# A seventh fast tile pair in the FFN's second product, with the weight sums of three tiles kept in DRAM

## The chip, the cores and the metric

The kernel runs on one core of a Trainium2 chip. The metric is the device time of one execution in microseconds; lower is better.

## The reference

The reference is one decoder block of a hybrid network on 256 tokens of width 1024: two token mixers and an output projection, then a SwiGLU FFN with a hidden width of 2816, each followed by a residual and a LayerNorm. All is float32. The change touches the FFN:

```python
h = jnp.einsum('bsd,df->bsf', x, w_ffn_in)
h_gate, h_up = jnp.split(h, 2, axis=-1)
y = jnp.einsum('bsf,fd->bsd', jax.nn.silu(h_gate) * h_up, w_ffn_down)
return layer_norm(DN_ALPHA * x + y, ln2_w, ln2_b)
```

## The kernel before

**Numbers in two parts.** TensorE multiplies in fp32r, which has fewer digits than float32. Each operand is therefore held as a high part h (a copy cast to fp32r) and a low part l (the operand less h), and a product is three matmuls: h with h, h with l, l with h. Weights come from DRAM in tiles of 128 x 2048 float32 (1 MB). For each tile, SP issues the load into a raw buffer (three of them, taken in turn), ScalarE casts it to `wh` (L204), and VectorE subtracts to make `wl` (L206). There are four h buffers and four l buffers, also taken in turn: the fifth tile can be cast only when TensorE has finished the first. `plan()` (L77) lists the tiles in their order, `loads` (L169) turns that into steps, and `fetch()` (L238) writes the steps into the program up to three ready tiles ahead of the one being used.

**The FFN's first product.** `ffn_step(j)` (L881) takes two feature blocks of the gate and two of the up half: two weight tiles, 32 matmuls each (L293 with 512 columns, L294 with 256). The results are copied out of PSUM by ScalarE (L887) and VectorE (L888), silu is taken and the activations are split into h and l. A scheduler sets the order of the steps up to `NF - 2 * ORDERED`; the last two steps and the second product are in the order in which they are written.

**The FFN's second product.** The hidden width makes eleven tile pairs q = 0 to 10: one weight tile of 256 rows by 1024 columns each. A plain pair (P) multiplies two row blocks by two token halves and two column halves: 8 products, 24 matmuls of 512 columns (`rows_pass`, L721). A fast pair (S) treats the tile as a 2 x 2 block matrix and needs 7 products, 21 matmuls (`fast`, L921). In exchange it needs sums of the tile's four blocks: `stage_fast` (L210) makes two sums on VectorE into `cst` (L221) and two into a tile called `sums` (L225, L226). Three of the blocks themselves ("corners") form one entry of the h and l buffers (L223, L227), and the four sums another (L232, L234). A fast pair also needs five sums of its activations (L896 to L899 and one existing block) and a split of 896 columns.

`DOWN = "SSPSSPSSPPP"` gives the order of the pairs: the fast ones take q = 2 to 7, the plain ones 0, 1, 8, 9, 10. In the program's own count the eleven weight tiles are numbers 66 to 76 in the order of `DOWN`; the names below carry these numbers. For the last three plain tiles, TensorE first does the products of token half 0, and those of half 1 at the end from the `held` tiles. The last PSUM piece is called `more`. After the last fast pair `into_residual` (L932) adds the shared results into the residual on VectorE (L935 to L944); in VectorE's order that stands behind the split of tile 76. Then come the LayerNorm of half 0 (L972 to L988) and of half 1 (`layer_norm`, L735; `more` is added at L746) and the stores.

Of the kernel before, what the change touches and what calls it, by code (L numbers as in the profile page):

```python
# [10 lines left out]
F32 = mybir.dt.float32  # L11
# [6 lines left out]
P = 128  # L18
T = 256
NT = T // P  # L20
D = 1024
# [3 lines left out]
NF = FF // P  # L25
# [10 lines left out]
HOLD_IN = 2  # L36
HOLD_DOWN = 3
ORDERED = 2
DOWN = "SSPSSPSSPPP"
FAST = tuple(range(2, 2 + DOWN.count("S")))  # L40
PLAIN = tuple(q for q in range(NF // 2) if q not in FAST)
SEQUENCE = [(FAST if s == "S" else PLAIN)[DOWN[:i].count(s)] for i, s in enumerate(DOWN)]

C_ID = 0
C_COS = C_ID + P
# [31 lines left out]
def plan():  # L77

    tiles = []

    def add(w, k0, kn, c0, n, held=False):
        tiles.append((w, k0, kn, c0 if isinstance(c0, tuple) else (c0,), n, held))

    def feat(w, c0, n):
        for c in range(c0, c0 + n, 256):
            add(w, 0, 8, c, 256)

    def tok(w, c0, n):
        for c in range(c0, c0 + n, 512):
            add(w, 0, 4, c, 512)  # L90
            add(w, 4, 4, c, 512)

    feat("w_in", 0, 1024)
    tok("w_in", 2048, 1024)
    tok("w_in", 3072, 1024)
    tok("w_in", 6144, 512)
    tok("w_in", 8192, 1024)
    for c in range(2):
        if c == 1:
            tok("w_in", 6144 + 512, 512)  # L100
        for j in range(2 * c, 2 * c + 2):
            feat("w_in", 5120 + j * 256, 256)
            feat("w_in", 4096 + j * 256, 256)
    tok("w_in", 7168, 1024)
    tok("w_branch_a", 0, 1024)
    tok("w_branch_b", 0, 1024)
    for k in range(0, KC, 2):
        add("w_out", k, 2, 0, 1024)
    for j in range(0, EARLY, 2):
        for k in range(0, KC, 4):  # L110
            add("w_ffn_in", k, 4, (j * P, FF + j * P), 256, j < HOLD_IN)
    for j in range(EARLY, NF, 2):
        add("w_ffn_in", 0, 8, j * P, 256)
        add("w_ffn_in", 0, 8, FF + j * P, 256)
    for q in SEQUENCE:
        add("w_ffn_down", 2 * q, 2, 0, 1024)
    return tiles
# [3 lines left out]
def hybrid_layer_kernel(ctx: ExitStack, tc, x, xw, vecs, bias, wts, ln1_w, ln1_b, ln2_w, ln2_b, consts, out):  # L121
    nc = tc.nc
    pool = lambda name, bufs, **kw: ctx.enter_context(tc.tile_pool(name=name, bufs=bufs, **kw))
    cp = pool("cp", 1)
    wraw = pool("wraw", 3)
# [8 lines left out]
    def slot(name, dt=F32):  # L134
        return big.tile([P, 2048], dt, tag="s8", name=name)

    def r32(ap):
        return ap.bitcast(F32)
# [28 lines left out]


    loads = []  # L169
    for i, (w, k0, k, _, _, held) in enumerate(plan()):  # L170
        fast = w == "w_ffn_down" and k0 // 2 in FAST
        loads += [(i, k, held, kind) for kind in (("corners", "sums") if fast else ("plain",))]
    ready = []
    corners = {}
    state = {"next": 0}

    def split(dst_h, dst_l, src):
        nc.scalar.copy(dst_h, src)
        nc.vector.tensor_sub(dst_l, src, r32(dst_h))
# [30 lines left out]
    def stage_fast(i, kind):  # L210


        view = lambda z: z.rearrange("p (b c) -> p b c", b=4)
        h = whi.tile([P, 2048], F32R, tag="h", name=f"wh{kind}{i}")
        l = wlo.tile([P, 2048], F32R, tag="l", name=f"wl{kind}{i}")
        if kind == "corners":
            b = view(wraw.tile([P, 2048], F32, tag="raw", name=f"raw{i}"))
            nc.sync.dma_start(b, view(wts[i]))
            y, z = corners[i] = [v.rearrange("p (b c) -> p b c", b=2) for v in (
                cst[:, C_COS:C_COS + D], cp.tile([P, D], F32, tag="mv1", name=f"sums{i}"))]  # L220
            nc.vector.tensor_sub(y, b[:, 1:3, :], b[:, 0:1, :].to_broadcast([P, 2, 512]))  # L221
            h, l = view(h)[:, 0:3, :], view(l)[:, 0:3, :]
            nc.scalar.copy(h, b[:, 1:4, :])  # L223
            yield
            nc.vector.tensor_add(z[:, 0, :], b[:, 2, :], y[:, 0, :])  # L225
            nc.vector.tensor_sub(z[:, 1, :], b[:, 3, :], z[:, 0, :])  # L226
            nc.vector.tensor_sub(l, b[:, 1:4, :], r32(h))  # L227
            yield
        else:
            h, l = view(h), view(l)  # L230
            for z, bs in zip(corners.pop(i), (slice(0, 2), slice(2, 4))):
                nc.scalar.copy(h[:, bs, :], z)  # L232
                yield
                nc.vector.tensor_sub(l[:, bs, :], z, r32(h[:, bs, :]))  # L234
                yield
        ready.append((h, l))

    def fetch(ahead=LOOKAHEAD):  # L238
        while state["next"] < len(loads) and len(ready) < 1 + ahead:
            list(stage())  # L240
        return ready.pop(0)
# [9 lines left out]
    cst = cp.tile([P, C_END], F32, tag="cst", name="cst")  # L251
# [153 lines left out]
    for j in range(4):  # L405
# [3 lines left out]
        for f in range(2):  # L409
            h = 2 * j + f  # L410
# [163 lines left out]
    mv1 = cp.tile([P, D], F32, tag="mv1", name="mv1")  # L574
# [205 lines left out]
    def fast_parts(i):  # L780
        if i == 0:
            tiles = [klp.tile([P, H * P], F32R, tag="kl", name="ash"), cp.tile([P, D], F32R, tag="bgr", name="asl")]
        else:
            both = slot(f"as{i}", F32R)
            tiles = [both[:, 0:1024], both[:, 1024:2048]]
        return [z[:, 0:7 * P].rearrange("p (b t) -> p b t", b=7) for z in tiles]
# [46 lines left out]
    with tc.manual_schedule(engines={ET.PE, ET.DVE, ET.Activation}):  # L833
# [3 lines left out]
        tiles = [(2 * q,) + fetch(0) for q in range(4)]  # L837
# [43 lines left out]
    def ffn_step(j):  # L881
# [17 lines left out]
        nc.vector.tensor_sub(z[:, 7, :], z[:, 3, :], z[:, 5, :])  # L899
        act_fast[q] = fast_parts(FAST.index(q))  # L900
        split(*act_fast[q], z[:, 1:8, :])
# [4 lines left out]
    with tc.manual_schedule(engines={ET.PE, ET.DVE, ET.Activation}):  # L906
# [9 lines left out]
        ends = dict(ktot=2 * PLAIN[-1] + 2)  # L916
        begins = {id(ps): SEQUENCE[0] for ps in (p2, p3, p4)}
        begins.update({id(wd0): PLAIN[0]})
        begins.update({id(ps): FAST[0] for ps in shared})

        def fast(q):  # L921
            ah, al = act_fast[q]
            for products in [((p1, 0, 0), (p2, 2, 2), (p3, 6, 1)),
                             ((p4, 1, 3), (p5, 3, 0), (p6, 4, 2), (p7, 5, 1))]:
                wh, wl = fetch()
                for ps, a, b in products:
                    stop = q == FAST[-1] and ps in shared
                    nc.tensor.matmul(ps, ah[:, a, :], wh[:, b, :], start=(q == begins[id(ps)]), stop=False)
# [18 lines left out]
        held = []  # L947
        for i, q in enumerate(SEQUENCE):
            if q in FAST:
# [4 lines left out]
            tile_q = [(2 * q,) + fetch()]  # L954
            if i < len(SEQUENCE) - HOLD_DOWN:
                for part in late:
# [5 lines left out]
        y = slot("y").rearrange("p (t d) -> p t d", t=NT)  # L962
        z, spare = [slot("z")[:, i:i + D] for i in (0, D)]
# [63 lines left out]
```

## Time and profile before

| What | Value |
|---|---|
| median of 3 runs | 496.59 us (495.87 to 496.79) |
| the profiled execution, own time | 496.43 us |
| its span | 494.6 us |
| TensorE busy (matmuls) | 486.1 us, 98% |
| VectorE busy | 395.8 us, 80% |
| ScalarE busy | 281.0 us, 57% |
| granted TensorE clock, mean | 0.996 |

The profile is of one execution. Times in it are microseconds from the start of the span. PE is TensorE's matmuls, PEld its weight loads, DVE VectorE, ACT ScalarE, POOL GpSimd, SP the engine that issues the loads. Matmuls are pipelined, so the busy times of neighbours overlap: how long one takes is read from the distance of their starts. Idle time of an engine is put down to what ended it. The chain that ended last is followed back from the last instruction. For a DMA issue, the number behind the size is the time to its landing in us.

### The profile page before, as it was taken

To read this page: it belongs to the slowest core of one execution; us is meant where nothing else is said; L and a number is where in the kernel's file an instruction comes from. 1 tells how busy PE (TensorE), PEld (TensorE's weight loads), DVE (VectorE), ACT (ScalarE), POOL (GpSimd) and SP (SyncE) were. 2 spreads that over 40 slices of the span, in tenths; PEclk is the share of its full clock that TensorE was granted. 3 is DMA by queue.
4 is the path that set the end of the run, shared out by engine and by line. 5 is a ranking of instruction groups with operands and counts; after the bars stand their busy time and mean duration, and the time that the engine had idled before them with its cause. 6 is when DMAs were issued, how large, how long until landed. Compare 5 with 4: busy or idle time off the path is not lost.

```text
span 494.6 us, 6732 instructions
## 1 busy us (share of the span) xinstructions
PE 486.1 (98%) x2662; PEld 421.8 (85%) x2662; DVE 395.8 (80%) x495; ACT 281.0 (57%) x355; POOL 33.7 (7%) x33
## 2 busy tenths in 40 slices
PE   9999999999999999999999999999999999999994
PEld 8899888888899888888888888888888888888883
DVE  4888799999868797876595778854887778889996
ACT  6696487435546676669653462544566655475621
POOL 0000000000003631240000000000000000000001
PEclk9999999999999999999999999999999999999998
DMA  8977426644442337358545456246455444365502
GB/s 310 420 265 278 170 94 246 221 162 170 171 170 88 131 133 285 105 171 311 185 171 172 168 176 239 95 175 250 172 186 219 189 171 170 113 238 201 215 1 85
DMA packets 14703, 92.65 MB, mean 187 GB/s; under 512 B 1744, under 2 KB 1744, under 8 KB 4944
## 3 DMA queue, kind: packets, MB, share of 16 engines
q1 hardware_dynamic: 13824, 89.08, 49.5%
q0 software_dynamic: 848, 3.15, 2.1%
q8 instruction: 21, 0.34, 0.3%
q14 instruction: 10, 0.08, 0.0%
HBM read 91.17 MB, written 1.05 MB: 186 GB/s over the span
## 4 chain that ended last, share of the span: by engine, by line
PE 87%; DVE 8%; DMA 2%; issue 1%; ACT 1%; DVEq 0%; ACTq 0%
PE fu L293 7%; PE fg L293 7%; PE fg L294 3%; PE fu L294 3%; PE mq L293 2%; PE mk L293 2%; PE sc L483 2%; PE hq L304 2%; PE hq L305 2%; PE hq L303 2%; PE hf L317 1%; PE za L341 1%; PE za L340 1%; PE ga L341 1%; PE mv L339 1%; PE gb L340 1%
## 5 line engine op out<-in xcount | busy, mean ns | idle before, releaser
L206 DVE TENSOR_TENSOR wl<-raw,wh 128x2048 fp32r<-128x2048 f32 (+1 forms) x72 | 164.5, 2291 | 53.9 <-ACT wh L204 53.6
L204 ACT CAST wh<-raw 128x2048 fp32r<-128x2048 f32 (+1 forms) x72 | 135.4, 1888 | 65.6 <-PE fg L293 11.5
L293 PE MATMUL fg<-x1p,wh 128*128 128x512 f32 x144 | 50.5, 394 | 0.0
L293 PE MATMUL fu<-x1p,wh 128*128 128x512 f32 x144 | 50.4, 394 | 0.0
L294 PE MATMUL fg<-x1p,wl 128*128 128x256 f32 x144 | 40.0, 278 | 0.0
L294 PE MATMUL fu<-x1p,wl 128*128 128x256 f32 x144 | 39.9, 277 | 0.0
L293 PEld LDWEIGHTS fu<-x1p,wh 128*128 128x128 f32 x144 | 27.0, 187 | 6.2
L293 PEld LDWEIGHTS fg<-x1p,wh 128*128 128x128 f32 x144 | 27.0, 187 | 6.1
L294 PEld LDWEIGHTS fg<-x1p,wl 128*128 128x128 f32 x144 | 27.1, 188 | 0.1
L294 PEld LDWEIGHTS fu<-x1p,wl 128*128 128x128 f32 x144 | 27.1, 188 | 0.0
L304 PE MATMUL hq<-xp,wh 128*128 128x256 f32 x64 | 18.1, 283 | 0.0
L305 PE MATMUL hq<-xp,wl 128*128 128x256 f32 x64 | 18.1, 283 | 0.0
L303 PE MATMUL hq<-xp,wh 128*128 128x256 f32 x64 | 18.1, 283 | 0.0
L293 PE MATMUL mk<-xp,wh 128*128 128x512 f32 x48 | 17.5, 402 | 0.0
L293 PE MATMUL mq<-xp,wh 128*128 128x512 f32 x48 | 17.2, 399 | 0.0
L485 DVE COPY_PREDICATED SD<-cst,sc 128x512 f32<-128x512 uint32 x14 | 14.9, 1072 | 1.2 <-PE sc L483 1.0
L733 PE MATMUL wp<-wh,ap 128*128 128x512 f32 (+1 forms) x40 | 14.9, 373 | 0.0
L732 PE MATMUL wp<-wl,ap 128*128 128x512 f32 (+1 forms) x40 | 14.9, 373 | 0.0
L731 PE MATMUL wp<-wh,ap 128*128 128x512 f32 (+1 forms) x40 | 14.9, 373 | 0.0
L521 POOL TENSOR_TENSOR ost<-ost,half 128x4 f32<-128x4 f32 x4 | 4.1, 1014 | 153.9 <-DVE ost L520 153.9
L294 PE MATMUL mk<-xp,wl 128*128 128x256 f32 x48 | 13.8, 288 | 0.0
L294 PE MATMUL mq<-xp,wl 128*128 128x256 f32 x48 | 13.6, 284 | 0.0
(329 smaller groups left out, 1319.8 us busy)
## 6 DMA issues: line engine op xcount, KB each, us to landing
raw<-in_wts_dram SPq DMA_DIRECT2D x76, 1024.0 KB, 4.8
xw<-in_xw_dram SPq DMA_DIRECT2D x6, 640.0 KB, 9.3
raw<-in_wts_dram SPq DMA_DIRECT2D x2, 512.0 KB, 12.2
xr<-in_x_dram POOLq DMA_DIRECT2D x1, 1024.0 KB, 5.9
wb<-in_ln_w_dram POOLq DMA_DIRECT2D x2, 512.0 KB, 5.5
wb<-in_ln_b_dram POOLq DMA_DIRECT2D x2, 512.0 KB, 7.5
cst<-in_consts_dram SPq DMA_DIRECT2D x1, 960.0 KB, 13.7
xw<-in_xw_dram SPq DMA_DIRECT2D x2, 384.0 KB, 4.0
```

The source lines that it names most:

```text
L204: nc.scalar.copy(h[:, ks, :], raw[:, ks, :])
L206: eng.tensor_sub(l[:, ks, :], raw[:, ks, :], r32(h[:, ks, :]))
L293: nc.tensor.matmul(ps, wh[:, k, wcol], a.both(k), start=(k == 0), stop=False)
L294: nc.tensor.matmul(ps[:, 0, :], wl[:, k, wcol], a[0, k, slice(0, T)], start=False, stop=(k == KC - 1))
L303: nc.tensor.matmul(ps, wh[:, k, wcol], ah[:, kk, :], start=(kk == 0), stop=False)
L304: nc.tensor.matmul(ps, wh[:, k, wcol], al[:, kk, :], start=False, stop=False)
L305: nc.tensor.matmul(ps, wl[:, k, wcol], ah[:, kk, :], start=False, stop=(kk == KC - 1))
L340: nc.tensor.matmul(pss[t], al[:, kk, ts], wh[:, k, :], start=False, stop=False)
L485: nc.vector.copy_predicated(later(SD, n, 4 * g, 4), m[:, None, :, :, :].to_broadcast([P, 4, nb, NT, n]), ps.rearrange("p a (b u i) -> p a ...
L731: nc.tensor.matmul(ps, lh(kk)[:, ts], wh[:, k, ns], start=(kk == first), stop=False)
L732: nc.tensor.matmul(ps, lh(kk)[:, ts], wl[:, k, ns], start=False, stop=False)
L733: nc.tensor.matmul(ps, ll(kk)[:, ts], wh[:, k, ns], start=False, stop=(kk == ktot - 1))
```

## The change

`DOWN` becomes `"SSTPSTSTPPP"`. There is a new kind of pair, T: fast like S, but with its four weight sums made earlier. The seven fast pairs are now q = 2 to 8 (8 was plain), the plain ones 0, 1, 9, 10. The T pairs are q = 4, 6 and 8, tiles 68, 71 and 73.

For each T tile an extra step of kind `ahead` is put behind the load of an up tile of the first product (those of blocks 6, 10 and 14): SP loads the tile into a raw buffer, VectorE makes the four sums, and GpSimd's queue writes them to a DRAM tile `spill`, 1 MB, in two DMAs. In the second product a T tile then has two loads, each with a raw buffer: three corner blocks (0.75 MB) and the four sums (1 MB). VectorE makes no sums for it; ScalarE casts and VectorE splits the sums in one instruction each of 2048 columns.

```diff
-DOWN = "SSPSSPSSPPP"
-FAST = tuple(range(2, 2 + DOWN.count("S")))
+DOWN = "SSTPSTSTPPP"
+SUMS_AFTER = (6,10,14)
+FAST = tuple(range(2, 2 + len(DOWN) - DOWN.count("P")))
...
+AHEAD = [q for q, s in zip(SEQUENCE, DOWN) if s == "T"]
...
+        if w == "w_ffn_in" and up[i] - NF in SUMS_AFTER:
+            loads.append((down[AHEAD[SUMS_AFTER.index(up[i] - NF)]], 2, False, "ahead"))
...
+    dram = pool("dram", 1, space=bass.MemoryType.DRAM)
+    spilled = {down[q]: dram.tile([P, 2048], F32, tag=f"sums{q}", name=f"spill{q}") for q in AHEAD}
...
+        def make_sums(b):
+            y, z = corners[i] = [v.rearrange("p (b c) -> p b c", b=2) for v in (
+                cst[:, C_COS:C_COS + D], cp.tile([P, D], F32, tag="mv1", name=f"sums{i}"))]
+            nc.vector.tensor_sub(y, b[:, 1:3, :], b[:, 0:1, :].to_broadcast([P, 2, 512]))
+            yield
+            nc.vector.tensor_add(z[:, 0, :], b[:, 2, :], y[:, 0, :])
+            nc.vector.tensor_sub(z[:, 1, :], b[:, 3, :], z[:, 0, :])
+
+        raw = lambda: view(wraw.tile([P, 2048], F32, tag="raw", name=f"raw{kind}{i}"))
+        if kind == "ahead":
+            b = raw()
+            nc.sync.dma_start(b, view(wts[i]))
+            list(make_sums(b))
+            for n, z in enumerate(corners.pop(i)):
+                nc.gpsimd.dma_start(view(spilled[i])[:, 2 * n:2 * n + 2, :], z)
+            return
...
         if kind == "corners":
+            b = raw()
+            n = 1 if i in spilled else 0
+            nc.sync.dma_start(b[:, n:4, :], view(wts[i])[:, n:4, :])
+            sums = make_sums(b) if n == 0 else iter(())
+            next(sums, None)
...
+        elif i in spilled:
+            z = raw()
+            nc.sync.dma_start(z, view(spilled[i]))
+            h, l = view(h), view(l)
+            nc.scalar.copy(h, z)
+            yield
+            nc.vector.tensor_sub(l, z, r32(h))
             yield
```

VectorE's order at the end of the second product, before: tile 73 with its sums, then the splits of the three last plain tiles and the residual.

```order
L221 TENSOR_TENSOR cst_85<-raw73_3928 128x1024
L225 TENSOR_TENSOR sums73_3930<-raw73_3928,cst_85 128x512
L226 TENSOR_TENSOR sums73_3930<-raw73_3928,sums73_3930 128x512
L227 TENSOR_TENSOR wlcorners73_3927<-raw73_3928,whcorners73_3926 128x1536
L234 TENSOR_TENSOR wlsums73_3961<-cst_85,whsums73_3960 128x1024
L234 TENSOR_TENSOR wlsums73_3961<-sums73_3930,whsums73_3960 128x1024
L206 TENSOR_TENSOR wl74_3977<-raw74_3975,wh74_3976 128x2048
L206 TENSOR_TENSOR wl75_3995<-raw75_3993,wh75_3994 128x2048
L206 TENSOR_TENSOR wl76_4010<-raw76_4008,wh76_4009 128x2048
L935 SCALAR_TENSOR_TENSOR x1_2434<-x1_2434,wp1_3746 128x512
```

The same place after, from tile 71's sums on:

```order
L260 TENSOR_TENSOR wlsums71_3919<-rawsums71_3920,whsums71_3918 128x2048
L227 TENSOR_TENSOR cst_90<-rawcorners72_3935 128x1024
L229 TENSOR_TENSOR sums72_3937<-rawcorners72_3935,cst_90 128x512
L230 TENSOR_TENSOR sums72_3937<-rawcorners72_3935,sums72_3937 128x512
L252 TENSOR_TENSOR wlcorners72_3934<-rawcorners72_3935,whcorners72_3933 128x1536
L267 TENSOR_TENSOR wlsums72_3956<-cst_90,whsums72_3955 128x1024
L267 TENSOR_TENSOR wlsums72_3956<-sums72_3937,whsums72_3955 128x1024
L252 TENSOR_TENSOR wlcorners73_3971<-rawcorners73_3972,whcorners73_3970 128x1536
L260 TENSOR_TENSOR wlsums73_3989<-rawsums73_3990,whsums73_3988 128x2048
L215 TENSOR_TENSOR wl74_4005<-raw74_4003,wh74_4004 128x2048
L215 TENSOR_TENSOR wl75_4023<-raw75_4021,wh75_4022 128x2048
L215 TENSOR_TENSOR wl76_4038<-raw76_4036,wh76_4037 128x2048
```

Tile 73 has lost its three sums and has one split of 2048 columns in place of two of 1024; the residual still stands behind tile 76.

SP's loads of the second product's last tiles, before:

```order
L218 DMA raw70_3824<-in_wts_dram 128x2048
L203 DMA raw71_3871<-in_wts_dram 128x2048
L218 DMA raw72_3891<-in_wts_dram 128x2048
L218 DMA raw73_3928<-in_wts_dram 128x2048
L203 DMA raw74_3975<-in_wts_dram 128x2048
L203 DMA raw75_3993<-in_wts_dram 128x2048
L203 DMA raw76_4008<-in_wts_dram 128x2048
```

And after:

```order
L245 DMA rawcorners70_3853<-in_wts_dram 128x2048
L245 DMA rawcorners71_3890<-in_wts_dram 128x1536
L256 DMA rawsums71_3920<-spill6_85 128x2048
L245 DMA rawcorners72_3935<-in_wts_dram 128x2048
L245 DMA rawcorners73_3972<-in_wts_dram 128x1536
L256 DMA rawsums73_3990<-spill8_86 128x2048
L212 DMA raw74_4003<-in_wts_dram 128x2048
L212 DMA raw75_4021<-in_wts_dram 128x2048
L212 DMA raw76_4036<-in_wts_dram 128x2048
```

Each load takes the raw buffer of the third load ahead of it. Tile 76 took that of tile 73 and now takes that of 73's sums; tile 75 took that of 72 and now takes that of 73's corners.

ScalarE's casts, which take the h buffers in this order, before:

```order
L204 CAST wh68_3768<-raw68_3767 128x2048
L223 CAST whcorners69_3785<-raw69_3787 128x1536
L232 CAST whsums69_3804<-cst_85 128x1024
L232 CAST whsums69_3804<-sums69_3789 128x1024
L223 CAST whcorners70_3822<-raw70_3824 128x1536
L232 CAST whsums70_3856<-cst_85 128x1024
L232 CAST whsums70_3856<-sums70_3826 128x1024
L204 CAST wh71_3872<-raw71_3871 128x2048
```

And after:

```order
L249 CAST whcorners68_3800<-rawcorners68_3802 128x1536
L258 CAST whsums68_3818<-rawsums68_3820 128x2048
L213 CAST wh69_3834<-raw69_3833 128x2048
L249 CAST whcorners70_3851<-rawcorners70_3853 128x1536
L265 CAST whsums70_3870<-cst_90 128x1024
L265 CAST whsums70_3870<-sums70_3855 128x1024
L249 CAST whcorners71_3888<-rawcorners71_3890 128x1536
L258 CAST whsums71_3918<-rawsums71_3920 128x2048
```

The plain tile has moved from place 68 to 69, tile 71 has turned from plain into T, and tile 71's sums stand four entries behind tile 69.

More of the change, by code (lines that the diff above doesn't have):

```diff
@@ L38 @@
 ORDERED = 2
-DOWN = "SSPSSPSSPPP"
-FAST = tuple(range(2, 2 + DOWN.count("S")))
+DOWN = "SSTPSTSTPPP"
+SUMS_AFTER = (6,10,14)
+FAST = tuple(range(2, 2 + len(DOWN) - DOWN.count("P")))
 PLAIN = tuple(q for q in range(NF // 2) if q not in FAST)
-SEQUENCE = [(FAST if s == "S" else PLAIN)[DOWN[:i].count(s)] for i, s in enumerate(DOWN)]
+SEQUENCE = [PLAIN[DOWN[:i].count("P")] if s == "P" else FAST[i - DOWN[:i].count("P")] for i, s in enumerate(DOWN)]
+AHEAD = [q for q, s in zip(SEQUENCE, DOWN) if s == "T"]
 C_ID = 0
@@ L169, in hybrid_layer_kernel @@
     loads = []
-    for i, (w, k0, k, _, _, held) in enumerate(plan()):
+    tiles = plan()
+    down = {t[1] // 2: i for i, t in enumerate(tiles) if t[0] == "w_ffn_down"}
+    up = [t[3][0] // P for t in tiles]
+    for i, (w, k0, k, _, _, held) in enumerate(tiles):
         fast = w == "w_ffn_down" and k0 // 2 in FAST
         loads += [(i, k, held, kind) for kind in (("corners", "sums") if fast else ("plain",))]
+        if w == "w_ffn_in" and up[i] - NF in SUMS_AFTER:
+            loads.append((down[AHEAD[SUMS_AFTER.index(up[i] - NF)]], 2, False, "ahead"))
     ready = []
     corners = {}
+    dram = pool("dram", 1, space=bass.MemoryType.DRAM)
+    spilled = {down[q]: dram.tile([P, 2048], F32, tag=f"sums{q}", name=f"spill{q}") for q in AHEAD}
     state = {"next": 0}
@@ L216, in stage_fast @@
         if kind == "corners":
[L217 to L221, printed above, removed]
+            b = raw()
[3 more added lines that the diff above has]
+            next(sums, None)
             h, l = view(h)[:, 0:3, :], view(l)[:, 0:3, :]
@@ L224, in stage_fast @@
             yield
-            nc.vector.tensor_add(z[:, 0, :], b[:, 2, :], y[:, 0, :])
-            nc.vector.tensor_sub(z[:, 1, :], b[:, 3, :], z[:, 0, :])
+            list(sums)
             nc.vector.tensor_sub(l, b[:, 1:4, :], r32(h))
+            yield
[4 more added lines that the diff above has]
+            nc.scalar.copy(h, z)
+            yield
+            nc.vector.tensor_sub(l, z, r32(h))
             yield
```

## The prediction

> **What bounds the kernel now.** I read the page's head first, then the busy time by stretches, then the chain that ended last, and only then single engines in the second product. In the head:
>
> ```profile
> span 494.6 us, 6732 instructions
> PE 486.1 (98%) x2662; PEld 421.8 (85%) x2662; DVE 395.8 (80%) x495; ACT 281.0 (57%) x355; POOL 33.7 (7%) x33
> ```
>
> TensorE is busy 98% of the span, so at first sight any matmul taken away is time won. The stretches (bounds in us; then PE, PEld, DVE, ACT, POOL busy, clock, DMA share, GB/s) show a second engine beside it:
>
> ```profile
> 330.00:390.00 60.00, 60.00 (x348) 52.54 (x347) 44.06 (x58) 34.74 (x44) 0.00 (x0) 1.00 0.54 193
> 410.00:430.00 20.00, 20.00 (x117) 17.48 (x116) 17.44 (x22) 10.36 (x17) 0.00 (x0) 1.00 0.38 141
> 430.00:440.00 10.00, 10.00 (x47) 8.31 (x46) 8.09 (x9) 6.08 (x6) 1.09 (x2) 1.00 0.61 210
> 440.00:470.00 30.00, 30.00 (x134) 24.81 (x133) 29.73 (x27) 18.00 (x14) 0.00 (x0) 1.00 0.60 211
> ```
>
> In the FFN's first product (the first two rows) VectorE has room; in the second product, which runs from 431, it is busy 29.73 of 30 us. The chain's last part says which of the two engines sets the end (start, us, what):
>
> ```profile
> 461.20 1.15 DVE cst L221
> ...
> 465.48 4.99 DMA raw<-in_wts_dram
> 470.57 1.92 ACT wh L204
> 472.51 2.29 DVE wl L206
> 474.81 0.60 DVE x L935
> ...
> 487.30 0.42 DVE y L746
> ```
>
> The end hangs on the last weight tile, number 76 (the eleven tiles of the second product are 66 to 76 in their order). Its load starts at 465.48, when VectorE's corners of tile 73 free a raw buffer; it lands at 470.47, is cast by ScalarE and split by VectorE, and then VectorE works through the residual and the norm, one instruction behind the other, to L746 at 487.30. TensorE comes in at the same moment:
>
> ```profile
> 435.77 0.39 PE L928 MATMUL wp<-whcorners,as 128*128 128x512 f32 x1
> ...
> 440.53 0.39 PE L731 MATMUL wp<-wh,ap 128*128 128x512 f32 x1
> ...
> 450.50 0.39 PE L930 MATMUL wp<-whsums,as 128*128 128x512 f32 x1
> ...
> 475.95 0.39 PE L731 MATMUL wp<-wh,ap 128*128 128x512 f32 x1
> ...
> 486.94 0.28 PE L733 MATMUL more<-wh,ap 128*128 128x256 f32 x1
> ```
>
> Its last matmul ends at 487.22, 0.08 us before L746, the first instruction that needs it. So two chains end together, and to win time both must get shorter. The rows of 0.39 us overlap: from 435.77 to 440.53 one fast tile's 21 matmuls took 4.76 us, 0.227 each.
>
> **The change, part by part.** TensorE: a plain tile costs 24 such matmuls, a fast one 21, so the seventh fast tile saves 3 x 0.227 = 0.68 us. TensorE's end would move to 486.54. That is all it can bring, since TensorE hardly waits anywhere now.
>
> VectorE in the second product, from these rows of tile 73 and of a plain tile's start:
>
> ```profile
> 461.12 1.22 DVE L221 TENSOR_TENSOR cst<-raw 128x1024 f32<-128x1024 f32 x1
> 462.37 0.69 DVE L225 TENSOR_TENSOR sums<-raw,cst 128x512 f32<-128x512 f32 x1
> ...
> 463.70 1.75 DVE L227 TENSOR_TENSOR wlcorners<-raw,whcorners 128x1536 fp32r<-128x1536 f32 x1
> 465.37 1.22 DVE L234 TENSOR_TENSOR wlsums<-cst,whsums 128x1024 fp32r<-128x1024 f32 x1
> ...
> 467.64 2.29 DVE L206 TENSOR_TENSOR wl<-raw,wh 128x2048 fp32r<-128x2048 f32 x1
> ...
> 474.72 0.68 DVE L935 SCALAR_TENSOR_TENSOR x<-x,wp 128x512 f32<-128x512 f32 x1
> ```
>
> A fast tile (S) takes 467.64 - 461.12 = 6.52 us, of which the sums are 463.70 - 461.12 = 2.58. With its sums read back (T) it takes 1.67 for the corners (463.70 to 465.37) and about 2.2 for one split of 2048 columns (the 2.29 row; the next instruction starts 2.2 after it, as 472.51 and 474.72 show): 3.9. Three T tiles save 7.7 us; the tile that turns from plain to T adds 1.7. VectorE has 6 us less to do there, and would be early if work were all that counts.
>
> It isn't, because a T tile uses two of the three raw buffers and two of the four h and l buffers, like two tiles. I follow it through, with ScalarE's casts:
>
> ```profile
> 434.23 1.04 ACT L232 CAST whsums<-sums 128x1024 fp32r<-128x1024 f32 x1
> 435.18 1.90 ACT L204 CAST wh<-raw 128x2048 fp32r<-128x2048 f32 x1
> 436.99 1.47 ACT L223 CAST whcorners<-raw 128x1536 fp32r<-128x1536 f32 x1
> ```
>
> Up to 440.53 (tiles 66 and 67) TensorE does what it does now. Then come 68 as T, to 445.29, and 69 as plain, to 450.73: 24 + 21 matmuls as before, the other way round. Ahead of it, VectorE does 68's corners at 436.7 to 438.4 (ScalarE's cast follows the sums of 67, at 435.2), 68's sums to 440.8 (cast to 438.5), 69 to 443.0; all are ready over 1.5 us before TensorE wants them. Tile 71's sums are the turning point. The entries in the h buffers are 69, 70 corners, 70 sums, 71 corners, 71 sums: the fifth needs the buffer of the first, so ScalarE can't cast 71's sums before TensorE has done tile 69, at 450.50 + 0.39 = 450.89. (Their load goes out with 69's buffer at 443.0 and lands by 449.1.) The cast ends at 452.8; VectorE has been idle since about 451.5 (70's load goes out at 438.4 with the buffer of 68's corners and lands by 443.3; 6.52 for tile 70 and 1.67 for 71's corners). It splits 71's sums from 452.85, starts tile 72 at 455.05 (loaded from 447.6, when 70's corners are done), the corners of 73 at 455.05 + 6.52 = 461.57, the sums of 73 at 463.24, and is done with them at 465.53. Tile 76 takes that raw buffer, three loads back: its load goes out at 465.55, against 465.48 now. Six us of VectorE's work are gone and the last load starts no sooner.
>
> It also travels in worse company. Now the load before it was issued at 458.96 by the same rule (corners of 72); after, tile 75 takes the buffer of 73's corners, free at 463.3, so the two loads are 2.2 us apart. Four such pairs of the trace, each with the landing time of the second under it:
>
> ```profile
> 33.67 3.21 SPq L203 DMA_DIRECT2D raw<-in_wts_dram  x2
> raw<-in_wts_dram SPq DMA_DIRECT2D x1, 1024.0 KB, 4.8
> 78.67 2.53 SPq L203 DMA_DIRECT2D raw<-in_wts_dram  x2
> raw<-in_wts_dram SPq DMA_DIRECT2D x1, 1024.0 KB, 5.2
> 332.20 3.05 SPq L203 DMA_DIRECT2D raw<-in_wts_dram  x2
> raw<-in_wts_dram SPq DMA_DIRECT2D x1, 1024.0 KB, 5.8
> 295.26 2.53 SPq L203 DMA_DIRECT2D raw<-in_wts_dram  x2
> raw<-in_wts_dram SPq DMA_DIRECT2D x1, 1024.0 KB, 6.1
> ```
>
> The two issues of a row take 0.33 us each, so they stood 2.2 to 2.9 us apart, and the second load took 4.8 to 6.1, 5.5 in the mean, against 4.99 for today's. I take 5.5: tile 76 lands at 471.05, 0.58 after now. The Trainium skill ("DMA: Bandwidth & Descriptors", Anatomy of one DMA) puts a DMA at about 2.0 us plus its bytes at 436 GB/s, by which a 1 MB load takes 4.4 us and one 2.2 us behind another an estimated 4.6; the sum would then be about -0.3. The rows disagree with it: no load quoted here took under 4.8.
>
> From the landing on, the way is as now: 470.47 to 474.72 is 4.25 us of cast and split, so L935 starts at 475.30, and the 12.58 us from there to L746 (474.72 to 487.30) are VectorE's own, so L746 comes at 487.88. TensorE wants tile 76 at 475.95 - 0.68 = 475.27 and gets it about 0.1 late, so its end is near 486.65, 1.2 us before VectorE asks. The 0.68 is won on TensorE and lost.
>
> First product: VectorE gets 3 x 2.58 = 7.7 us of sums between about 329 and 385; it was idle for 15.9 of the 60 us in 330:390. Tile pair 8's activations turn from plain to fast:
>
> ```profile
> L179 DVE TENSOR_TENSOR as<-room,as 128x896 fp32r<-128x896 f32 x2 | 2.2, 1082 | 0.0
> L896 DVE TENSOR_TENSOR room<-room 128x128 f32<-128x128 f32 x2 | 0.6, 292 | 0.1
> ```
>
> Four adds of 0.29 and a split of 1.08 in place of one of 512 columns (0.69, as L225) make 1.6 us, against 2.56 idle in 410:430 and 1.9 in 430:440. I put both at nothing: they sit under TensorE's matmuls. The cover is the four h buffers: a cast starts when TensorE frees a buffer, and its tile is wanted three tiles later. A tile is 32 matmuls, 348 in 60 us, so 5.5 us; 16.5 less 1.9 for the cast and 2.3 for the split leaves 12.3. The extra load pushes the next one back by at most one tile, 5.5, and VectorE's sums stand ahead of a split for 2.6: 8.1 of 12.3. If the cover fails, TensorE stalls, one for one. SP's extra loads and GpSimd's spills go out in order; nothing waits behind the spills on GpSimd until wb2's loads at 430, and the next sums over `cst` come 22 us later.
>
> The sum against the profiled execution, 496.43 us (span 494.6 and 1.8 around it): +0.07 + 0.51 = +0.58, 497.0. The median of the runs shown is 0.16 higher, 496.59, so **497.2**. Between the ends of the landing (4.8 and 6.1) it is -0.12 to +1.18.
>
> **The rivals.** A measurement of this kernel can tell about 0.2% (1.0 us) from no change: its three runs span 495.87 to 496.79.
>
> First, the last load is early after all: VectorE has 6 us less to do, and if tile 71's sums aren't held by the h buffer, or the loads don't collide, L935 starts by 474.0 and TensorE's 0.68 comes through in full. For it: the work is gone; against it: the order of the buffers. It gives 495.9, and anything up to +0.1 on the way. Even that lies within 0.2%; faster by more needs a saving that I can't find, or the runs' scatter.
>
> Second, on the other side, the collision of the last two loads is dearer. It decides from a landing of 5.9 us (then the sum passes 1.0). One row above is over that, and this one, a raw load beside two loads of GpSimd's queue:
>
> ```profile
> raw<-in_wts_dram SPq DMA_DIRECT2D x1, 1024.0 KB, 7.2
> wb<-in_ln_b_dram POOLq DMA_DIRECT2D x1, 512.0 KB, 7.7
> ```
>
> 7.2 gives +0.07 + 2.2 = 2.3, 498.9.
>
> Third, the first product's cover fails: spills and extra loads slow the weight loads beside them. The Trainium skill says (same page, "Issuing engines are not separate DMA queues") that DMAs of all issuers share the 16 engines and interleave; the 7.2 row beside GpSimd's loads agrees. Such a load is 2.4 us late, which with 8.1 makes 10.5 of the 12.3: no stall, unless two fall together, then some 2 us, 498.6.
>
> That the change doesn't do what it says, the order of the matmuls excludes: three fewer.
>
> **How the numbers follow.** The forecast (sum +0.1 to +1.0) has 0.50; the first rival 0.24; the second 0.20; the third 0.06. Slower by over 0.2% are the last two, and 0.02 of the forecast's upper edge: 0.28. Faster by over 0.2% is left with 0.06 of the first rival, for scatter on top of its full gain. The rest, 0.66, is within 0.2%. The range runs from the first rival's full gain, 495.9, to the dear collision, 498.9.
>
> **What would show it.** Right: in the changed profile the chain's end is again load, cast, split, L935 and the norm on VectorE; the cast of tile 71's sums waits for TensorE's matmuls of tile 69; the last two loads are issued 2 to 3 us apart and the last takes 5.2 us or more; TensorE's last matmul ends a microsecond before the add of `more`. Wrong: the last load issued clearly before 465; L746 starting right at TensorE's end; or TensorE idle between 330 and 430, or at tiles 68 to 73.

## The result and the profile after

| What | Before | After |
|---|---|---|
| median of 6 runs each | 496.57 us (495.87 to 496.79) | 499.31 us (498.70 to 499.55) |
| ratio, 95% interval | | 1.0055 (1.0045 to 1.0065) |
| the profiled execution, own time | 496.43 us | 498.98 us |

The change costs 2.74 us in the medians and 2.55 us between the two profiled executions. The forecast was 497.2, so more than two microseconds are missing in its sum. The head of the page of the changed kernel:

```profile
span 496.9 us, 6763 instructions
PE 487.8 (98%) x2659; PEld 422.6 (85%) x2659; DVE 400.5 (81%) x501; ACT 282.5 (57%) x354; POOL 36.5 (7%) x39
```

TensorE has three matmuls fewer, as meant, and is busy 1.7 us longer. The end of the chain that ended last (start, us, what):

```profile
463.83 1.67 DVE wlcorners L252
465.50 2.21 DVE wlsums L260
467.73 5.34 DMA raw<-in_wts_dram
473.16 1.92 ACT wh L213
475.11 2.29 DVE wl L215
477.40 0.60 DVE x L968
```

It is the chain that the prediction drew: corners and sums of tile 73, the load of tile 76, cast, split, residual (L968 is the old L935). It is only late as a whole. Where it became late is read from TensorE's first matmul of the second product and from the first instruction that needs its last matmul, `y<-y,more` (L746 before, L779 now). The first product's end in the timeline of before:

```profile
430.96 0.40 PE L928 MATMUL wp<-whcorners,ash 128*128 128x512 f32 x1
```

And, in the timeline of after, the same matmul, TensorE's last one and the add:

```profile
432.73 0.39 PE L961 MATMUL wp<-whcorners,ash 128*128 128x512 f32 x1
...
488.34 0.28 PE L766 MATMUL more<-wh,ap 128*128 128x256 f32 x1
...
489.89 0.40 DVE L779 TENSOR_TENSOR y<-y,more 128x256 f32<-128x256 f32 x1
```

The second product begins 432.73 - 430.96 = 1.77 us later. From there to the add it took 487.30 - 430.96 = 56.34 us and takes 489.89 - 432.73 = 57.16, 0.82 more. Together 2.59: the whole loss of the profiled execution (2.55), in two parts. The smaller part is the forecast's (+0.58). The larger lies in the first product, which the forecast put at nothing.

The first product does not wait. This is one stretch of it, before (bounds; PE, PEld, DVE, ACT, POOL busy with their counts; clock, DMA share, GB/s):

```profile
370.00:430.00 60.00, 60.00 (x348) 52.48 (x348) 48.01 (x67) 34.86 (x46) 0.00 (x0) 1.00 0.47 174
```

And after:

```profile
370.00:430.00 60.00, 60.00 (x342) 52.05 (x341) 50.76 (x74) 35.02 (x46) 1.06 (x2) 1.00 0.58 206
```

TensorE is busy for 60.00 of 60 us in both, at the full granted clock, and does 342 matmuls where it did 348. The Trainium skill ("Perfetto Trace Analysis", Identifying the Most-Contended Engine) warns that the busy share of matmuls says little, because they are pipelined, and that the busy share of the weight loads says more. The two rows agree: PE's column doesn't move, PEld's falls from 52.48 to 52.05.

How much longer a matmul takes is read from starts. The 97th matmul of the gate and up tiles `fg` and `fu` (the first feature blocks, `fe`, come ahead of them) and the one 448 later, in the timeline of before:

```profile
347.76 0.39 PE L293 MATMUL fu<-x1p,wh 128*128 128x512 f32 x1
...
425.41 0.39 PE L293 MATMUL fu<-x1p,wh 128*128 128x512 f32 x1
```

The same two, after:

```profile
347.93 0.40 PE L326 MATMUL fu<-x1p,wh 128*128 128x512 f32 x1
...
427.08 0.40 PE L326 MATMUL fu<-x1p,wh 128*128 128x512 f32 x1
```

77.65 us have become 79.15. Start to start, sixteen matmuls (eight of 512 columns, eight of 256) take 2.773 to 2.774 us in each of the 28 blocks between these rows before, and 2.819 to 2.831 in each after. It isn't a stall here and there, and it goes on to 430, long after the last of the three new steps (its last write is issued at 382.02 and lands 8.5 us later). The slow distance has a pattern: from one 512-column matmul to the next it is 349, 350 and 361 ns in turn, while none of these steps before takes over 350. It begins at one place. There two transposes, `fet`, go through TensorE; they turn activations of the first feature blocks, which are made with the tokens on the rows. In the timeline of before:

```profile
338.50 0.40 PE L293 MATMUL fg<-x1p,wh 128*128 128x512 f32 x1
338.73 0.38 PE L827 MATMUL fet<-cst,se 128*128 128x128 f32 x2
338.87 0.49 PE L293 MATMUL fu<-x1p,wh 128*128 128x512 f32 x1
```

And after:

```profile
339.11 0.28 PE L327 MATMUL fg<-x1p,wl 128*128 128x256 f32 x1
339.23 0.38 PE L860 MATMUL fet<-cst,se 128*128 128x128 f32 x2
339.37 0.48 PE L326 MATMUL fu<-x1p,wh 128*128 128x512 f32 x1
```

The scheduler has put the pair three matmuls later, since the first new step (behind tile 6) delays on VectorE what the pair transposes: the product `se` starts there at 334.81 before and at 335.44 after, behind the first two of the new step's three instructions. Behind the pair TensorE turns to the up tile for 32 matmuls and only then comes back to the gate tile; these 32 have moved with the pair, and nothing else in TensorE's order of the first product has. Up to the pair both kernels run at 2.773; behind it the changed one runs at 2.82 to 2.83. From the first `fg` matmul (330.64 and 330.68) to the second product it is 100.32 us before and 102.05 after.

### The profile page after: what moved, and what is told of

The parts are those of the page before. It is cut to its first block, busy times and chain, and to the rows that moved or that the text cites. A ratio compares the mean times of both kernels' runs of the same rounds, so it can differ in the third digit from the quotient of the medians.

```text
span 496.9 us, 6763 instructions
## 1 busy us (share of the span) xinstructions
PE 487.8 (98%) x2659; PEld 422.6 (85%) x2659; DVE 400.5 (81%) x501; ACT 282.5 (57%) x354; POOL 36.5 (7%) x39
## 4 chain that ended last, share of the span: by engine, by line
PE 91%; DVE 5%; ACT 1%; DMA 1%; issue 1%; DVEq 0%; ACTq 0%
PE fu L326 7%; PE fg L326 7%; PE fg L327 3%; PE fu L327 3%; PE mq L326 2%; PE mk L326 2%; PE sc L516 2%; PE hq L337 2%; PE hq L338 2%; PE hq L336 2%; PE hf L350 1%; PE za L373 1%; PE mv L372 1%; PE za L374 1%; PE mv L374 1%; PE ga L374 1%
## 5 line engine op out<-in xcount | busy, mean ns | idle before, releaser
L215 DVE TENSOR_TENSOR wl<-raw,wh 128x2048 fp32r<-128x2048 f32 (+1 forms) x71 | 162.3, 2291 | 49.1 <-ACT wh L213 48.9
L213 ACT CAST wh<-raw 128x2048 fp32r<-128x2048 f32 (+1 forms) x71 | 133.6, 1888 | 69.0 <-PE gb L373 11.2
L326 PE MATMUL fu<-x1p,wh 128*128 128x512 f32 x144 | 51.4, 399 | 0.0
L372 PE MATMUL mv<-wh,xp 128*128 128x512 f32 x32 | 13.0, 406 | 0.0
L374 PE MATMUL za<-wl,yah 128*128 128x512 f32 x32 | 12.8, 400 | 0.0
L372 PE MATMUL za<-wh,yah 128*128 128x512 f32 x32 | 12.7, 396 | 0.0
```

Of the source, the lines that this page charges most:

```text
L213: nc.scalar.copy(h[:, ks, :], raw[:, ks, :])
L215: eng.tensor_sub(l[:, ks, :], raw[:, ks, :], r32(h[:, ks, :]))
L326: nc.tensor.matmul(ps, wh[:, k, wcol], a.both(k), start=(k == 0), stop=False)
L372: nc.tensor.matmul(pss[t], ah[:, kk, ts], wh[:, k, :], start=(kk == 0), stop=False)
L374: nc.tensor.matmul(pss[t], ah[:, kk, ts], wl[:, k, :], start=False, stop=(kk == KC - 1))
```

## The experiments

The theory: TensorE has two steady distances for the same stream of matmuls, and where a pair of transposes cuts into the stream can decide which one follows; that costs 1.8 us. The rest, 0.8 to 1.1 us, is the second product's end, by the chain that was predicted. The rivals: the new loads and spills slow TensorE's reads down; or the second product's loss has another cause than the turn of the raw buffers.

**sums_8_10_14: the first step two tiles later, so that TensorE's order in the first product is that of before.**

```diff
-SUMS_AFTER = (6,10,14)
+SUMS_AFTER = (8,10,14)
```

> The changed kernel with its first sums step two blocks later (behind up tile 8 instead of 6). TensorE's matmuls in the first product then stand in the order of the kernel before: the two last transposes of the early part stand behind the 13th matmul of gate block 6, a 512-column one, and not behind its 16th, a 256-column one. Theory (rhythm): the matmuls of the first product fall into one of two steady rhythms, 346.7 or 353.3 ns for a pair of 512 and 256 columns, and the place of those transposes chose the slow one. Then 16 matmuls take 2.773 us here as before, the second product starts at 431.0, and the time is 499.3 - 1.8 = 497.5 us. Rival (load): the extra loads, spills and VectorE sums slow TensorE; they are all still here, so 16 matmuls take 2.82 to 2.83 us and the time stays at 499.3.

497.29 us (496.79 to 498.05, 11 runs) beside 496.23, ratio 1.0024 (1.0015 to 1.0032). The stretch from 370 to 430:

```profile
370.00:430.00 60.00, 60.00 (x347) 52.45 (x347) 51.99 (x76) 35.33 (x47) 1.07 (x2) 1.00 0.59 213
```

With all three sums, their loads and their spills, sixteen matmuls take 2.773 us again, and from the first `fg` matmul to the second product, at 430.84, it is 100.32 us as in the kernel before. What is left, 1.06 us, arises behind 430.84.

**ahead_only: the change's first half alone.** The three sums are made and written to DRAM, and the second product is that of before and never reads them.

```diff
-DOWN = "SSTPSTSTPPP"
+DOWN = "SSPSSPSSPPP"
...
-AHEAD = [q for q, s in zip(SEQUENCE, DOWN) if s == "T"]
+AHEAD = [4, 5, 6]
...
-            n = 1 if i in spilled else 0
+            n = 0
...
-        elif i in spilled:
+        elif False:
```

> The order of pairs of the kernel before, with three sums steps in the first product (behind up tiles 6, 10, 14) that are spilled and never read: the change's first half alone. TensorE's order in the first product is that of the changed kernel. Rhythm: 2.82 to 2.83 us for 16 matmuls, the second product starts 1.8 us late, time 496.6 + 1.8 = 498.4. Load: the same, 498.4 (this run doesn't tell the two apart). Second rival (second product): the loss lies in the T tiles alone, the first product is as before, 496.6.

498.09 us (497.75 to 498.38, 6 runs), ratio 1.0035 (1.0023 to 1.0048). 341 matmuls from 370 to 430, 102.05 us from the first `fg` matmul to the second product, which begins at 433.03 (some 0.3 of it late already at 330), then 56.29 us to the add (56.34 before). The first half costs 1.86 us with nothing changed in the second product.

**kick_behind_h and kick_behind_l: the changed kernel with two transposes of the identity more**, into a PSUM tile that nothing reads, in the tenth gate tile: in one kernel between a matmul of 512 columns and its partner of 256, in the other behind that partner.

```diff
                 nc.tensor.matmul(ps, wh[:, k, wcol], a.both(k), start=(k == 0), stop=False)
+                if name == "fg10" and f == 0 and k == 6:
+                    kt = aux.tile([P, 2, P], F32, tag="aux", name="kick")
+                    for u in range(2):
+                        nc.tensor.transpose(kt[:, u, :], ident, ident)
```

> The changed kernel with two transposes of the identity into an unused PSUM tile put into gate block 10, between the 512-column and the 256-column matmul of k = 6 (about 389 us); their result is read by nobody. Rhythm: the distance of matmuls may change at that place and stays changed to the end of the first product; if it falls from 353 to 347 ns a pair, the first product wins 0.8 us from there on, less 0.3 for the transposes. Load: the distance is the same ahead of and behind the transposes, and the time is 0.3 us longer.

> The same two transposes one matmul later, behind the 256-column matmul of k = 6. Rhythm: the distance may change or not, and need not do so as in the other place; a change in either of the two shows a rhythm that history sets. Load: no change of the distance in either, 0.3 us longer.

One run each: 498.26 and 498.86 us. The stretch behind the kick (it comes at about 367, not at 389 as expected), in kick_behind_h:

```profile
370.00:430.00 60.00, 60.00 (x348) 52.91 (x347) 51.41 (x75) 35.26 (x47) 1.06 (x2) 1.00 0.58 207
```

And in kick_behind_l:

```profile
370.00:430.00 60.00, 60.00 (x341) 52.04 (x340) 50.55 (x74) 35.16 (x46) 1.07 (x2) 1.00 0.57 206
```

The loads and the spills are the same in both, yet behind one kick the distance is 2.773 us at once and to the end, and behind the other nothing changes: from the first `fg` matmul to the second product 101.04 us and 102.26, against 102.05 without a kick. That speaks against the load and for a state.

**before_kick_h and before_kick_l: the same two kicks in the kernel before**, which has no sums ahead, no spills and no extra loads.

> The kernel before with two transposes of the identity matrix more (into a PSUM tile that nothing reads), in the first product's tenth gate tile between a matmul of 512 columns and its partner of 256, where the changed kernel's twin of this run found its way back to 2.773 us per 16 matmuls. No weight sums, no spills, nothing else. Theory (TensorE's distance between matmuls is a state that the place of such a pair of transposes decides, whatever else the kernel does): behind a matmul of 512 columns the pair leaves the distance at 2.773 us per 16, and the time grows by the pair itself, 0.1 to 0.3 us: 496.5 to 496.8. Rival (the slower distance comes of the sums and their spills): 2.773 too, so this run is the control of the next.

> The same one matmul later, behind the matmul of 256 columns, the place at which the change puts its own pair of transposes and after which its distance was 2.82 to 2.83 us per 16. Theory: the distance turns to 2.82 to 2.83 us per 16 from about 367 us to the end of the first product, some 23 times 16 matmuls by 0.046 to 0.058 us: 1.1 to 1.3 us more, 497.4 to 497.8, with no weight sums in the kernel at all. Rival (the sums, their loads and spills slow TensorE down): 2.773 us throughout, 496.5 to 496.8. A third way: the place decides only together with the state before it, and this pair does nothing here though the theory of a state holds; then the distance stays at 2.773 as well, and this run does not tell.

497.92 us (497.43 to 498.44, 6 runs; ratio 1.0030, 1.0019 to 1.0042) and 496.74 (496.50 to 497.50, 10 runs; 1.0009, 1.0000 to 1.0018). The stretch in before_kick_h:

```profile
370.00:430.00 60.00, 60.00 (x342) 52.01 (x341) 46.67 (x65) 34.48 (x45) 0.00 (x0) 1.00 0.48 176
```

The expectation had the two places the wrong way round: the kick behind 512 columns, which was to be the control, turned the distance to 2.82 to 2.83, and the one behind 256 left it at 2.773. The main point is the stronger for it. The kernel before, with two transposes more and nothing else, loses 1.46 us (497.92 less 496.46). From the first `fg` matmul to the second product its profiled execution took 101.77 us, and that of before_kick_l 100.54, against 100.32; so the pair itself takes some 0.22, and the slower distance the rest. Sums, spills and loads aren't needed for it, and neither is a change in the order of the kernel's own matmuls. In these four runs a pair behind 512 columns turned the state, whichever it was, and one behind 256 kept it. That is no rule: the changed kernel's own `fet` stands behind 256 and turned it, and the one of before stands behind 512 and didn't.

**down_ttst: sums_8_10_14 with another order of the second product**: the second and the third T pair each change places with the S pair ahead of them (so the last T pair stands one place further from the end, not the three tiles that the expectation names).

```diff
-DOWN = "SSTPSTSTPPP"
+DOWN = "SSTPTSTSPPP"
```

> sums_8_10_14 with one edit: the order of the second product's tiles is S S T P T S T S P P P instead of S S T P S T S T P P P, so that the loads of sums kept in DRAM (which need no corners' correction on VectorE and only one load each less than a plain tile) come earlier and the last T pair stands three tiles further from the end. Same number of products, same sums. Theory (the rotation of the raw buffers near the end sets the time): the last load, tile 76's, then waits for another tile's buffer and has its neighbour some 4 us ahead instead of 2.2; worked through by the rotation it is issued at 464.2 to 465.0 and lands in 4.8 us, at 469.0 to 469.8, its split ends 0.6 us or more ahead of the kernel before, and TensorE's 0.7 us shows: about 495.5 to 495.9 beside 496.2 to 496.6. Rival: the order of the tiles does not matter as every tile takes its turn of three buffers anyway, and the time stays 1.0 us over the kernel before, at about 497.3.

495.67 us (494.84 to 496.09, 11 runs) beside 496.42, ratio 0.9982 (0.9973 to 0.9991): the expectation held, and this version is faster than both kernels. The last load goes out at 464.94 and lands in 4.99 us. In the timeline of VectorE and TensorE at the end:

```profile
474.19 0.68 DVE L968 SCALAR_TENSOR_TENSOR x<-x,wp 128x512 f32<-128x512 f32 x1
...
486.51 0.28 PE L766 MATMUL more<-wh,ap 128*128 128x256 f32 x1
486.83 0.42 DVE L779 TENSOR_TENSOR y<-y,more 128x256 f32<-128x256 f32 x1
```

L968 begins 0.53 sooner than L935 did, and the add stands right behind TensorE's last matmul (486.51 + 0.28). TensorE's matmuls of the second product span 486.51 - 431.27 = 55.24 us against 486.94 - 430.96 = 55.98: the saving of three matmuls, at last visible.

**raw75_own and raw75_slot: sums_8_10_14 with a buffer of its own for tile 75**, so that the three raw buffers' turn is shorter by one.

```diff
-        raw = view(wraw.tile([P, 2048], F32, tag="raw", name=f"raw{i}"))
+        raw = view(slot(f"raw{i}") if i == 75 else
+                   wraw.tile([P, 2048], F32, tag="raw", name=f"raw{i}"))
```

> sums_8_10_14 (the seventh tile pair, with the weight sums made after the first product's tiles 8, 10 and 14) with one edit: the corners of tile 75 get a buffer of their own instead of one of the three that the raw weight tiles take in turn. Theory: what is left of the loss, 1.06 us in that run, is the second product's end: three raw buffers in turn hold tile 76's load until tile 73's sums have been cast and split (465.79 there), and VectorE's 12.58 us after that tile's split end the kernel. With 75 out of the turn, tile 76 takes the buffer of tile 73's corners, free some 2 us sooner (about 463.3), and 75 is loaded some 4 us ahead of it with no neighbour, so that tile 76 lands by 468.2 to 469 and its split ends by 473; then VectorE's tail is late by nothing and TensorE's three times 0.227 us saved show: 0.7 us under the kernel before, about 495.5 to 495.9 beside 496.2 to 496.6. Rival: the raw buffers' turn is not what holds the end (TensorE, or the 12.58 us themselves, started by something else), and the time stays 1.0 us over the kernel before, at about 497.3.

In raw75_own the condition was `i == len(tiles) - 2`, and the list `tiles` has another length by the time tile 75 is loaded, so tile 75 kept its turn and the run is sums_8_10_14 once more: 497.41 us (496.86 to 498.10, 11 runs), ratio 1.0021 (1.0012 to 1.0030). It shows that the 1.0 us repeat, and no more.

> raw75_own did not hold the edit it was to hold: tile 75 kept its place in the turn of three raw buffers (its load still waits for tile 73's corners, at 463.41), so that run is sums_8_10_14 once more. Here tile 75 has a buffer of its own in the program; its load stands ahead of tile 69's on SP and waits for TensorE alone, so it is issued some 20 us sooner. Theory (the turn of the raw buffers sets the end): tile 76 then takes the buffer of tile 73's corners at about 463.4 instead of that of its sums at 465.6 to 465.8, has no neighbour and lands in 4.7 to 4.9 us, by 468.3; its split ends by 473, some 2 us sooner than in the kernel before (474.72), TensorE is late by nothing and its 0.7 us show: about 495.5 to 495.9, with TensorE's last matmul 55.2 us after its first of the second product. Rival: the end hangs on something else than that turn: 1.0 us over the kernel before, at about 497.3, with VectorE's line 968 at 475.4 to 475.8 as before.

497.58 us (496.45 to 497.98, 11 runs), ratio 1.0022 (1.0013 to 1.0031): not the expected gain. The buffer is free as soon as the first product ends, and the load went out beside tile 69's. In TensorE's timeline, at the corners of tile 72:

```profile
460.11 0.39 PE L962 MATMUL wp<-whcorners,as 128*128 128x512 f32 x1
461.60 0.50 PE L963 MATMUL wp<-wlcorners,as 128*128 128x512 f32 x1 [1.11 <-DVE wlcorners L253]
```

With two loads in flight from 431 on, those that followed took 6.0 to 7.5 us instead of 4.2 to 6.2, VectorE got its tiles late, and here TensorE's next matmul came after 1.49 us instead of 0.23. The run put a new wait in place of the old one and says nothing on the turn.

**raw75_late: the same, with tile 75's load held back** by a one-column copy on VectorE behind the split of tile 72's corners.

```diff
-        raw = view(wraw.tile([P, 2048], F32, tag="raw", name=f"raw{i}"))
+        raw = view(state["raw75"] if i == 75 else
+                   wraw.tile([P, 2048], F32, tag="raw", name=f"raw{i}"))
...
             nc.vector.tensor_sub(l, b[:, 1:4, :], r32(h))
+            if i == 72:
+                state["raw75"] = slot("raw75")
+                nc.vector.tensor_copy(state["raw75"][:, 0:1], r32(l[:, 0, 0:1]))
```

> raw75_slot with one edit: tile 75's load waits for a one-column copy on VectorE that follows the split of tile 72's corners, so that it is issued beside tile 74's (459.7 to 460.0) and not beside tile 69's at 430.8, where the two loads took 7.6 and 9.6 us and TensorE stood still for 1.5 us at 460. Theory (the turn of the raw buffers sets the end of sums_8_10_14): tile 76's load goes out at about 463.6 instead of 465.8; with three loads in flight it lands in 5.5 to 7.2 us, at 469.1 to 470.8, VectorE's line 968 begins at 472.5 to 474.6 instead of 475.75, and the time falls from 497.3 to 495.5 to 496.4. Rival (the turn is not what holds the end): line 968 at 475.5 or later and 497.3.

496.66 us (495.35 to 497.44, 11 runs), ratio 1.0006 (0.9996 to 1.0015); the profiled execution took 495.88. The chain's end:

```profile
461.92 1.68 DVE wlcorners L253
...
463.62 6.40 DMA raw<-in_wts_dram
470.12 1.92 ACT wh L214
472.07 2.29 DVE wl L216
474.36 0.59 DVE x L972
```

Tile 76 now follows the corners of tile 73, not the sums, and is issued at 463.62 instead of 465.79; with three loads in flight it takes 6.40 us and still lands 1.5 us sooner. The residual starts at 474.27 (expected 472.5 to 474.6; 475.75 in sums_8_10_14), and TensorE's second product spans 55.24 us without a stall. The instants are the theory's. The median is 0.3 above the upper end of the expected times; the runs scatter over 2 us, the profiled execution is the second fastest of the eleven, and where the slower ones lose their time no trace shows.

**ttst_6_10_14: down_ttst's order with the change's own places for the sums.**

```diff
-SUMS_AFTER = (8,10,14)
+SUMS_AFTER = (6,10,14)
```

> The changed kernel with down_ttst's order of the second product (S S T P T S T S P P P), but with the sums made after tiles 6, 10 and 14 as in the change, so that TensorE's first product has the change's order. Theory (two separate losses, the first product's distance between matmuls and the second product's end): sixteen matmuls of the first product take 2.82 to 2.83 us as in the change, the second product begins 1.8 us later than in down_ttst and then takes 55.2 us, with no loss at the end: 495.67 + 1.8, about 497.3 to 497.6. Rival: the two hang together (the slower first product is what makes the second late for its loads, or the order of the second changes the first): with sixteen matmuls in 2.773 us, 495.5 to 495.9, or with the loss at the end kept, 498.5 to 499.3.

497.51 us (496.85 to 499.13, 11 runs), ratio 1.0025 (1.0016 to 1.0034). 341 matmuls from 370 to 430; the second product spans 55.43 us. From the first `fg` matmul to the second product it is 102.05 us again. The first part of the loss is there and the second is gone: the two are separate, and the time is 1.84 us above down_ttst's, where 1.8 was expected.

## Why the prediction was wrong

**The step that failed** is the one on the first product: "I put both at nothing: they sit under TensorE's matmuls." The cover itself held. Raw loads beside the spills did take long, as the third rival had it. Three issues of the changed kernel, at 336.8 (with the spill beside it), 359.4 and 381.7 us:

```profile
raw<-in_wts_dram SPq DMA_DIRECT2D x1, 1024.0 KB, 8.9
spill<-sums POOLq DMA_DIRECT2D x1, 512.0 KB, 8.8
...
raw<-in_wts_dram SPq DMA_DIRECT2D x1, 1024.0 KB, 8.3
...
raw<-in_wts_dram SPq DMA_DIRECT2D x1, 1024.0 KB, 8.2
```

Each had another raw load in flight too, issued 0.8 to 1.3 us ahead. The latest was some 4.1 us late (8.9 less 4.8), where the third rival had reckoned with 2.4, and 8.1 + 4.1 = 12.2 is just inside the 12.3 of the cover. Yet TensorE waited for none of them: from 339.8 to the end of the product each of its steps from one 512-column matmul to the next takes 349, 350 or 361 ns. What the step left out is that VectorE's new work moves an instruction in TensorE's own order. The pair `fet` needs VectorE's `se`; that comes later in the scheduler's order, and the pair lands three matmuls further on. The forecast had looked at the order only near the end. What hangs on this is 1.73 us of the 1.77: the order of before gives 100.32 us with the sums (sums_8_10_14, down_ttst), and the order of after 102.05 with either second product (ahead_only, ttst_6_10_14). That a pair of transposes is enough to turn the distance is shown by before_kick_h.

The page of before held a sign of it. The same two lines of code serve a product of the mixers (`mq`) and the FFN's first product (`fg`):

```profile
L293 PE MATMUL fg<-x1p,wh 128*128 128x512 f32 x144 | 50.5, 394 | 0.0
...
L293 PE MATMUL mq<-xp,wh 128*128 128x512 f32 x48 | 17.2, 399 | 0.0
```

394 against 399 ns for the same shape, with no idle time in either. On the page of the changed kernel the FFN's rows read as those of the mixers did:

```profile
L326 PE MATMUL fu<-x1p,wh 128*128 128x512 f32 x144 | 51.4, 399 | 0.0
L326 PE MATMUL fg<-x1p,wh 128*128 128x512 f32 x144 | 51.3, 398 | 0.0
```

In the starts of before, the mixers' matmuls of this kind (`mq` and `mk`) hold the slow distance at 165.6 to 171, 193.1 to 196.6 and 199.6 to 207, with 2.82 to 2.83 us per sixteen, and the fast one at 188 to 191, with 0.345 to 0.347 us for each pair of 512 and 256 columns. Both distances had been in the kernel all along; in the FFN it was the fast one throughout. The Trainium skill ("TensorE: Matmul & The Clock Gate", Back-to-back issue gap) says that in a stream of weight loads and matmuls the distance is set by both. The rows don't speak against that, but don't show it either: 0.347 and 0.353 us were measured for a pair of 512 and 256 columns, both above an estimated 0.325 that the section's formula for an isolated matmul (columns at 2.4 GHz and 2.5 ns) gives without weight loads.

**TensorE's saving**, 0.68: right. 0.74 without a stall (down_ttst, raw75_late); in the changed kernel 0.37, as stalls of 0.28 at 474.3 and a few longer gaps eat the rest.

**VectorE's work**: the 6 us less of the prediction is a slip. Before, there were six S pairs; now there are four S and three T, so two pairs turn from S into T and save 2 x 2.6 = 5.2, the third T pair was plain and costs 1.7 more, and 3.5 are left. From the second product's start to the residual VectorE's instructions add up to 42.87 us before and 39.13 after, 3.7 less. The forecast's sum doesn't use the 6 us; the first rival leaned on it.

**Tile 71's sums wait for tile 69**: right in its mechanism, and 0.4 short. ScalarE's and VectorE's timelines of the changed kernel:

```profile
453.07 1.91 ACT L258 CAST whsums<-rawsums 128x2048 fp32r<-128x2048 f32 x1 [2.80 <-PE wp L766]
...
455.01 2.29 DVE L260 TENSOR_TENSOR wlsums<-rawsums,whsums 128x2048 fp32r<-128x2048 f32 x1 [1.60 <-ACT whsums L258]
```

From the second product's start the cast comes at 20.34 us; forecast were 450.89 - 430.96 = 19.93. TensorE's last matmul of tile 69 starts at 452.30 and lasts 0.39, so 0.38 us pass from its end to the cast. The forecast let the cast begin at that end. That moves the last load to 467.73 - 432.73 = 35.00 us behind the start, against 34.52 before: +0.48, where +0.07 was said.

**The last load's company**: right. The two were issued at 465.52 and 467.73, 2.21 apart as forecast, and the second took 5.34 us (5.5 said). In sums_8_10_14 and raw75_own it took 5.70 and 5.57. The mean of the four pairs was a good price. The 4.4 us that the prediction quotes beside it come from a fit that the Trainium skill ("DMA: Bandwidth & Descriptors", Anatomy of one DMA) gives for DMAs issued by GpSimd; this load is SP's, and took 5.34.

**VectorE's tail**: right to the hundredth: L968 starts at 477.31 in VectorE's timeline, and 489.89 - 477.31 = 12.58 us. TensorE's end is 1.27 us ahead of the add (1.2 said).

So behind the start of the second product the sum is +0.48 + 0.35 = +0.83 for +0.58, and ahead of it +1.77 for nothing. The range's upper end, 498.9, was reached through rivals that didn't occur: the collision cost no 7.2 us, and no load made TensorE stall in the first product.

Each sign that the prediction named for being right came out: the same chain, the cast behind tile 69, the last two loads 2.21 us apart, TensorE's end a microsecond ahead of the add. None of those for being wrong did; the 0.28 us of stalls at 474.3 stand behind tile 73. All these signs look at waits and at the end, and a first product that runs slower without waiting shows in none.

Two things stay open: what in the stream decides which distance TensorE takes, and what in the hardware holds it there. The runs show that a pair of transposes can turn it and that it then stays to the end of the product. In the change itself the pair moved together with the 32 matmuls behind it, so that the pair alone turned it there is likely, but not shown apart from them.

## What to carry to other kernels

When a change adds work on a second engine, compare the whole order of the bounding engine, not only at the place of interest: a shift by three places cost more here than everything that the change was about. Count matmuls per microsecond instead of trusting a busy share of 98%, and where one line of code shows two mean durations in one profile, ask what sets them apart. When buffers are taken in turn, the order of their users decides when the last load starts; trying another order (down_ttst) turned a loss of 1.1 us into a gain of 0.75.

## What the runs showed of the hardware

- A stream of fp32r matmuls of 512 and 256 columns, each with its own weight load, has two steady distances at the same granted clock of 1.00: 2.773 us and 2.82 to 2.83 us per sixteen. Each was held for over 60 us. In the slow one every third pair of 512 and 256 columns takes 360 or 361 ns and the others 349 or 350; in the fast one they take 343 to 350. Two transposes of 128 x 128 changed from either to the other (kick_behind_h, before_kick_h), or left it (the other two).
- Most 1 MB loads took 4.6 to 5.0 us with no other near them (in the kernel before one took 6.0, at 450.22, and one 7.0, at 357.69). As the second of two 2.2 to 2.9 us apart they took 4.8 to 6.1, with three in flight for a part of the time 6.4 to 6.8, and 6.5 to 9.4 beside GpSimd's second write of a spill and another load (changed kernel and sums_8_10_14). These writes, 0.5 MB from SBUF to DRAM, took 7.2 to 9.3 us, the first ones of the spills 2.9 to 5.3.
- From the modelled end of a matmul to the cast on ScalarE that waits for it, 0.38 us passed, and 0.36 in sums_8_10_14. From ScalarE to VectorE it was 0.02 to 0.03.
